# A float32 hybrid decoder trunk: state-space gates and products put in another order, attention in time halves, and the last projection in token layout

## The chip, the core and the metric

The kernel runs on one core of a Trainium2 chip. The metric is device time in microseconds, the median of several executions. Five engines work beside each other and each takes its instructions in order: TensorE (PE, matrix products into PSUM banks; PEld is its weight load), VectorE (DVE), ScalarE (ACT), GpSimd (POOL) and SyncE (SP), which here mostly issues DMA transfers.

## The reference, cut to what matters

256 tokens, width 1024, two layers, all float32:

```python
x = x + mamba2_mixer(rms_norm(x))          # state-space mixer, 8 groups of 4 heads
x = x + conv_ffn(rms_norm(x))              # 1024 -> 2 x 2816 -> 1024
k, v = shared_kv(rms_norm(x))              # 3 dilation groups (1, 4, 16), 2 KV heads each
x = x + dilated_attention(rms_norm(x), k, v)   # 8 heads a group, merged by softmax denominators
x = x + conv_ffn(rms_norm(x))
return rms_norm(x)

# mixer: z, xBC, dt = split(h @ w_in); xBC = silu(causal_conv4(xBC))
#   y = ssd(xs, dt, a, B, C) + d_skip * xs; y = group_norm(y * silu(z)); return y @ w_out
# ffn: u = causal_conv3(h @ w_up); return (silu(gate) * val) @ w_down
```

Three groups of keys with one softmax over them all is what the merge by denominators amounts to, and the kernel computes it so: a query has 256 columns for dilation 1 and 64 of its own residue class modulo 4 for each of the dilations 4 and 16, with a mask over all 384.

## The kernel before, in words

Activations stand as `[feature, token]`. Every large product is made of three one-pass products of rounded halves: weights `w = wh + wl` (`split`, L91 to L98: ScalarE rounds, L95, VectorE takes the difference, L97) and activations `x = xh + xl` (`hi_lo`, L168 and L169). `mm3` and `tile_a` (L242 to L244) have the weights stationary and 256 tokens moving; `tile_b` (L262 to L264) has 128 tokens stationary and 256 weight columns moving. Small products (state space, scores, values) are plain float32: each shows as two instructions in the trace.

`Weights` loads 1 MB pieces in the order of `seq` through three `raw` buffers and six pairs of `wh`/`wl`, one piece ahead. TensorE's order is the program's order (`manual_schedule`). The other engines' queues are put in order by a scheduler at build time, by readiness and program order; `seq(...)` chains some ScalarE passes.

Mixer: gates `z` (8 tiles of 256 columns, `z_mm`; three ahead of the groups and the rest as `ZAT` says), then for each of 8 groups two tiles each of `xs` and of B and C (`conv_mm`, 24 products a tile), their convolution (`conv_post`, VectorE taps L286) and Silu. A group's state-space work: `ssd_b` transposes `xs` (`px`) and makes `xdt`; `ssd_a` makes B x C (`pg`); `ssd_m` multiplies it into the decay `dec` (GpSimd); `ssd_c` makes `yo` and `py` and, over VectorE, GpSimd and ScalarE, the gated and normalised `y2` (`rs` is its scale); `ssd_d` transposes `y2` (`pt`) into the halves `yy`. `operands` makes the normalised halves `xnh`, `xnl`; `chunk_sums` the running sums (`pac`). `res_proj` multiplies by `w_out`, `w_down` or `w_o`, adds into `X` and feeds the next norm's operands (`Stream`); `hooks` runs leftover work between its steps; a step of `w_o`, or of the first four tiles of `w_out`, is three products of 256 columns. `late` are the operands that it takes last.

Attention: queries of the dilated groups stand by class `t % 4`. A head is three q tiles (`q_tile`, 24 products each), `scores` (two halves of 128 queries, 384 keys), softmax on VectorE and ScalarE, `p_transpose` (six 128-wide transposes) and `values`; in the loop over heads `p_transpose` and `values` run two heads behind, `scores` one:

```python
q_tile(h, hs[h], 0);  p_transpose(h - 2, hs[h - 2])
q_tile(h, hs[h], 1);  scores(h - 1, hs[h - 1])
q_tile(h, hs[h], 2);  values(h - 2, hs[h - 2])
```

The end: the last `w_down` leaves `[feature, token]`, its squares are summed over partitions by TensorE (`fss`, L934), 16 transposes turn it (`fin`, L927), four passes scale it and four DMAs write it.

Of the kernel before, what the change touches and what calls it, by code (L numbers as in the profile page):

```python
# [12 lines left out]
T = 256  # L13
D = 1024
# [17 lines left out]
_PRM = [("a_norm", 8), ("kv_norm", 8), ("b_norm", 8), ("ffn_norm0", 8), ("ffn_norm1", 8),  # L32
        ("final_norm", 8), ("ssm_norm", 16), ("dt_bias", 32), ("a_log", 32), ("dskip", 32),
# [3 lines left out]
_ATT = [("mask", 768), ("cos", 256), ("sin", 256), ("cosp", 256), ("sinp", 256)]  # L37
# [15 lines left out]
def trunk(ctx, tc, a, out):  # L53
# [46 lines left out]
    class Weights:  # L100


        def __init__(self):
# [5 lines left out]
            self.seq += [(("w_v", p), a["w_v"][p], 1024) for p in (1, 2, 0)]  # L109
# [27 lines left out]
        def begin(self, load, operand):  # L137

            _, src, m = self.seq[0]
            raw = wp.tile([128, 2048], F32, tag="raw", bufs=RB, name="raw")  # L140
            whl = [[wp.tile([128, 1024], F32R, tag=t, bufs=WB, name=t) for t in ("wh", "wl")]
                   for _ in range(2)]
            for i in range(4):
                c = slice(512 * i, 512 * i + 512)
                load(i)
                SP.dma_start(out=raw[:, c], in_=src[:, c])
            SP.dma_start(out=wdt.rearrange("p k h -> p (k h)"), in_=a["w_dt"])
            for i in range(4):
# [26 lines left out]

    class Stream:


        def __init__(self, ws):
            self.ws = ws  # L180
            self.h = []
            self.l = []
            for i in range(len(ws)):
# [20 lines left out]
    class Norm:  # L204


        def __init__(self, acc):
            self.acc = acc

        def stats(self):  # L210
            acc = self.acc
            ss = ps.tile([128, 512], F32, tag="t3", name="ss")
# [41 lines left out]
    def tile_b(po, units, xh, xl, n, c, ks=range(KT), clear=True, **kw):  # L254

        t = slice(c * 128, c * 128 + 128)
        kper = KT // len(units)
# [48 lines left out]
    def operands():  # L306
# [3 lines left out]
        for i in range(2):  # L310
            t = act.tile([128, 4, T], F32, tag=f"dec{2 + i}", name="xnt")
            for k in range(4):
                ACT.activation(out=t[:, k, :], in_=X[:, 4 * i + k, :], func=AF.Copy,
                               scale=P("a_norm")[:, 4 * i + k:4 * i + k + 1])
            for k in range(0, 4, 2):
                d, o = t[:, k:k + 2, :], slice(4 * i + k, 4 * i + k + 2)
                POOL.tensor_tensor(out=d, in0=d, in1=nm.row2, op=ALU.mult)
# [5 lines left out]
    W.fetch(2)  # L323
# [7 lines left out]
    sq += [wk.tile([128, 2 * T], F32, tag="zs", bufs=4, name="sq2") for _ in range(3)]  # L331
# [18 lines left out]
    def z_mm(g, c, **kw):  # L350
        st = sts[g]
        if "poz" not in st:
            st["poz"] = ps.tile([128, 2, T], F32, tag="t4", name="poz") if g == 2 else acc_bank()
            st["uz"] = W.get("w_z", g)
        tile_b(st["poz"][:, c, :], st["uz"], *xn[g > 2], 256, c, **kw)

    for k in range(0, KT, 2):
        for c in range(2):
            z_mm(0, c, ks=range(k, k + 2), clear=c == 0, skip_group_check=True)
# [5 lines left out]
    nm.stats()  # L365
    z_mm(1, 0)
    pdq = ps.tile([128, 512], F32, tag="t2", name="pdq")
    for c in range(2):
        PE.transpose(pdq[:, 32 * c:32 * c + 32], dtT[:, 128 * c:128 * c + 128], ident[0:32, 0:32])
    nm.bcast()  # L370
    z_mm(1, 1)
    col = nm.col
    W.fetch(4)
# [87 lines left out]

    def z_post(g):
        st, po = sts[g], sts[g]["poz"]
        zs = wk.tile([128, 2, T], F32, tag="zs", bufs=4, name="zs")
        if g < 3:
            for c in range(2):
                seq(out=zs[:, c, :], in_=po[:, c, :], func=AF.Silu, scale=col[:, c:c + 1])
        else:
            seq(out=zs, in_=po, func=AF.Silu)
        st["z"] = zs  # L470

    def ssd_a(g):
# [11 lines left out]

        if g == NG - 1:
            ssd_m(g)
# [28 lines left out]
    def ssd_c(g):  # L515
# [9 lines left out]
        y2 = wk.tile([128, 2, T], F32, tag="B", bufs=3, name="y2")  # L525
# [5 lines left out]
        POOL.tensor_tensor(out=y2, in0=xd, in1=st["z"], op=ALU.mult)  # L531
# [21 lines left out]
    for g in range(2):  # L553
        z_post(g)
    for c in range(2):
        z_mm(2, c)
    z_post(2)

    for g in range(NG):
        late = g > 1 and g - 1 not in ZAT  # L560
        conv_mm(g, "xs", 0)
        if late:
            ssd_c(g - 2)
        conv_mm(g, "xs", 1)
# [4 lines left out]
        conv_post(g, "xs")  # L569
        conv_silu(g, "xs")  # L570
        if g > 1 and not late:
            ssd_d(g - 2)
        conv_mm(g, "bc", 0)
# [3 lines left out]
        conv_mm(g, "bc", 1)  # L577
        conv_post(g, "bc")
        if g == 0:
            decay(0, sts[g]["end"])  # L580
# [486 lines left out]
```

## Time and profile before

| | |
|---|---|
| median of three runs | 794.57 us (794.43 to 795.48) |
| profiled execution | 796.08 us, span 794.3 us |
| mean granted TensorE clock | 0.993 |
| instructions | 14954 |

The span runs from the first to the last instruction of the profiled execution; its time has some 1.8 us beside the span. Busy time of TensorE runs from a product's start to its modelled end, so products that follow each other overlap; their cost is read from start to start. The granted clock is a share of 2.4 GHz.

### The profile page before, as it was taken

What the parts mean: (1) busy time and instruction counts of PE and PEld (TensorE: products, weight loads), DVE (VectorE), ACT (ScalarE), POOL (GpSimd) and SP (SyncE); (2) the same over time, 40 slices, a digit from 0 to 9 for tenths busy, and PEclk for the clock granted to TensorE, in tenths of its full rate; (3) what the DMA queues carried; (4) which work ended last, traced back from release to release, by engine and by line L of the source; (5) the groups of instructions that cost most, each with busy time, mean ns of one, the idle gap of its engine ahead of it and who ended that gap; (6) DMA issues with size and microseconds to landing.
All of it is one profiled execution on the core that took longest, in us unless ns stands there. A gap on an engine that the chain in (4) does not pass through costs nothing.

```text
span 794.3 us, 14954 instructions
## 1 busy us (share of the span) xinstructions
PE 774.3 (97%) x5992; PEld 742.7 (94%) x5992; DVE 619.5 (78%) x1004; ACT 478.6 (60%) x806; POOL 160.6 (20%) x141
## 2 busy tenths in 40 slices
PE   8999799999999999999999999999999999999997
PEld 7898799999989999999889999999999999999886
DVE  5888979788496999887677598878668999887551
ACT  7846568777375776655555446555466766565441
POOL 0323436543324400000011032211124300000010
PEclk9999989999999999999999999999999999999999
DMA  8484543363454366554556644334325465545521
GB/s 296 169 321 165 203 153 106 109 212 113 154 201 171 106 238 213 186 183 163 196 179 225 222 160 156 115 129 159 108 61 205 149 226 209 199 160 177 177 85 53
DMA packets 22886, 135.31 MB, mean 170 GB/s; under 512 B 2529, under 2 KB 4097, under 8 KB 8865
## 3 DMA queue, kind: packets, MB, share of 16 engines
q1 hardware_dynamic: 21616, 130.14, 47.0%
q10 hardware_dynamic: 1200, 4.23, 1.5%
q8 instruction: 47, 0.77, 0.4%
q14 instruction: 23, 0.18, 0.1%
HBM read 132.75 MB, written 1.61 MB: 169 GB/s over the span
## 4 chain that ended last, share of the span: by engine, by line
PE 75%; DVE 11%; POOL 4%; ACT 4%; issue 3%; DMA 2%; SPq 0%; DVEq 0%; ACTq 0%; POOLq 0%
PE po L242 15%; PE po L243 15%; PE po L244 15%; PE po L625 12%; PE po L627 6%; DVE wl L97 6%; PE po L633 4%; DVE cv L286 2%; PE s L854 1%; DVE xl L169 1%; POOL rs L537 1%; PE py L524 1%; PE op L888 1%; ACT wh L95 1%; PE op L892 1%
## 5 line engine op out<-in xcount | busy, mean ns | idle before, releaser
L97 DVE TENSOR_TENSOR wl<-raw,wh 128x1024 fp32r<-128x1024 f32 (+1 forms) x242 | 307.8, 1278 | 64.0 <-ACT wh L95 63.1
L95 ACT CAST wh<-raw 128x1024 fp32r<-128x1024 f32 (+1 forms) x242 | 247.7, 1034 | 170.5 <-PE po L243 87.0
L243 PE MATMUL po<-xnl,wh 128*128 128x256 f32 x800 | 227.0, 284 | 1.1 <-DVE xnl L319 1.1
L242 PE MATMUL po<-xnh,wh 128*128 128x256 f32 x800 | 227.0, 284 | 0.0
L244 PE MATMUL po<-xnh,wl 128*128 128x256 f32 x800 | 227.0, 284 | 0.0
L242 PEld LDWEIGHTS po<-xnh,wh 128*128 128x128 f32 x800 | 152.8, 191 | 0.3 <-issue 0.2
L243 PEld LDWEIGHTS po<-xnl,wh 128*128 128x128 f32 x800 | 151.2, 189 | 1.3 <-DVE xnl L319 1.3
L244 PEld LDWEIGHTS po<-xnh,wl 128*128 128x128 f32 x800 | 151.2, 189 | 0.1
L625 PE MATMUL po<-gp,wh 128*128 128x512 f32 x352 | 123.3, 393 | 0.0
L286 DVE SCALAR_TENSOR_TENSOR cv<-po,prm,cv 128x255 f32<-128x255 f32 (+2 forms) x232 | 105.8, 476 | 14.1 <-ACT cv L282 12.6
L242 PE MATMUL po<-xh,wh 128*128 128x256 f32 x400 | 115.0, 288 | 0.0
L243 PE MATMUL po<-xl,wh 128*128 128x256 f32 x400 | 113.2, 283 | 0.5 <-DVE xl L169 0.5
L244 PE MATMUL po<-xh,wl 128*128 128x256 f32 x400 | 113.0, 283 | 0.0
L627 PE MATMUL po<-gp,wl 128*128 128x256 f32 x352 | 98.5, 280 | 0.0
L625 PEld LDWEIGHTS po<-gp,wh 128*128 128x128 f32 x352 | 66.0, 187 | 15.4
L242 PEld LDWEIGHTS po<-xh,wh 128*128 128x128 f32 x400 | 76.3, 191 | 0.6
L243 PEld LDWEIGHTS po<-xl,wh 128*128 128x128 f32 x400 | 76.0, 190 | 0.7 <-DVE xl L169 0.7
L244 PEld LDWEIGHTS po<-xh,wl 128*128 128x128 f32 x400 | 75.9, 190 | 0.0
L627 PEld LDWEIGHTS po<-gp,wl 128*128 128x128 f32 x352 | 66.2, 188 | 0.0
L202 POOL TENSOR_TENSOR sqacc<-sqacc,sq 128x256 f32<-128x256 f32 x21 | 19.9, 946 | 217.0 <-ACT sq L201 216.7
L647 DVE TENSOR_TENSOR X<-po,X 128x256 f32<-128x256 f32 x52 | 20.9, 420 | 24.4 <-PE po L627 17.4
L202 POOL TENSOR_TENSOR facc<-facc,sq 128x256 f32<-128x256 f32 x6 | 4.5, 752 | 157.6 <-ACT sq L201 157.6
(207 smaller groups left out, 1270.4 us busy)
## 6 DMA issues: line engine op xcount, KB each, us to landing
raw<-w_up SPq DMA_DIRECT2D x44, 1024.0 KB, 4.8
raw<-w_down SPq DMA_DIRECT2D x16, 1024.0 KB, 4.8
raw<-w_xs SPq DMA_DIRECT2D x8, 1024.0 KB, 4.8
raw<-w_bc SPq DMA_DIRECT2D x8, 1024.0 KB, 4.8
raw<-w_out SPq DMA_DIRECT2D x8, 1024.0 KB, 4.8
raw<-w_q SPq DMA_DIRECT2D x8, 1024.0 KB, 5.1
raw<-w_z SPq DMA_DIRECT2D x7, 1024.0 KB, 6.2
raw<-w_down SPq DMA_DIRECT2D x8, 768.0 KB, 4.2
```

Source lines behind the costliest of these rows:

```text
L95: ACT.copy(out=wh[:, :n], in_=raw)
L97: DVE.tensor_tensor(out=wl[:, :n], in0=raw, in1=wh[:, :n].bitcast(F32), op=ALU.subtract)
L169: DVE.scalar_tensor_tensor(out=xl, in0=x, scalar=w, in1=xh.bitcast(F32), op0=ALU.mult, op1=ALU.subtract)
L202: POOL.tensor_tensor(out=acc, in0=acc, in1=sq, op=ALU.add)
L242: PE.matmul(po, lhsT=wh, rhs=xh, start=start, stop=False, **kw)
L243: PE.matmul(po, lhsT=wh, rhs=xl, start=False, stop=False, **kw)
L244: PE.matmul(po, lhsT=wl, rhs=xh, start=False, stop=stop, **kw)
L286: r = DVE.scalar_tensor_tensor(out=dst[:, i, s:], in0=u[:, i, :T - s], scalar=w[i][:, taps - 1 - s:taps - s], in1=dst[:, i, s:], op0=ALU.m ...
L625: PE.matmul(p.rearrange("p c t -> p (c t)"), lhsT=wh[:, c], rhs=y.rearrange("p c t -> p (c t)"), start=st, stop=False, skip_group_check=True)
L627: PE.matmul(p[:, 1, :], lhsT=wl[:, c], rhs=y[:, 0, :], start=False, stop=sp, skip_group_check=True)
L633: PE.matmul(p[:, o, :], lhsT=l[:, c], rhs=y[:, x, :], start=st and q == 0 and not o, stop=sp and q == 2, skip_group_check=True)
L647: DVE.tensor_tensor(out=x, in0=by_class(y) if perm else y, in1=x, op=ALU.add)
```

## The change

- Gates: 0 to 3 are made first, as two pairs of 512 columns from the unnormalised halves; 4 to 7 follow groups 1, 3, 5 and 7. VectorE makes the normalised operand in one pass a tile (ScalarE and GpSimd did in two).
- Mixer: `ssd_a` and `ssd_b` of group g-1 stand behind both B/C tiles of group g; `ssd_c(g-2)` and `ssd_d(g-3)` between them. `chunk_sums` stands behind the B/C tiles of group 0. Decays are loaded and exponentiated in pairs. `y2` lives in its group's `dec` buffer.
- V of the two dilated groups is one product 512 wide. Queries stand by class within each half of 128 tokens, keys in natural order (read with a stride of four columns); the first half's scores have 192 columns instead of 384 and two transposes instead of three; `values` handles two heads at once and writes its bank with a stride of four columns.
- `w_o`: hooks at 4, 7, 17 and 21 steps.
- The last projection has tokens stationary and 512 columns moving, so that its result stands as `[token, feature]`. `X` is transposed during the second up-projection (`turn`), the squares are summed by ScalarE's accumulator, and the outputs go out by two queues.

```diff
-ZAT = {0: 3, 2: 4, 5: 5, 6: 6, 7: 7}
-SSM = [("z", 0), ("z", 1), ("z", 2)]
+ZAT = {1: 4, 3: 5, 5: 6, 7: 7}
+SSM = [("z2", i) for i in range(4)]
 for _g in range(NG):
-    SSM += [("xs", _g), ("bc", _g)] + ([("z", ZAT[_g])] if _g in ZAT else [])
+    SSM += [("xs", _g), ("bc", _g)] + ([("z", ZAT[_g] - 4)] if _g in ZAT else [])
...
+    def z_pair(i, ks, po):
+        us = sum((W.get("w_z2", 2 * i + j) for j in sorted({k // 4 for k in ks})), [])
+        for k in ks:
+            for c in range(2):
+                tile_b(po[c], {k // 2: us[k // 2 - ks[0] // 2]}, *xn[0], 512, c, ks=[k])
...
+        tile_b(st["poz"][:, c, :], st["uz"], *xn[1], 256, c)
+    poz = [[ps.tile([128, 512], F32, tag=f"t{4 + c}", name="poz") for c in range(2)],
...
+        y2 = act.tile([128, 2, T], F32, tag=f"dec{g}", name="y2")
...
     for g in range(NG):
-        late = g > 1 and g - 1 not in ZAT
...
+        for i in range(2):
+            conv_mm(g, "xs", i)
+        conv_post(g, "xs")
+        conv_silu(g, "xs")
+        conv_mm(g, "bc", 0)
+        if g > 2:
+            ssd_d(g - 3)
+        if g > 1:
             ssd_c(g - 2)
-        conv_mm(g, "xs", 1)
+        conv_mm(g, "bc", 1)
...
+        if g and g % 2 == 0:
+            decay_load(g)
+            decay_load(g + 1)
+        if g % 2 == 0:
+            decay(g, sts[g]["end"])
+            decay(g + 1, sts[g]["end"])
         if g:
             ssd_b(g - 1)
             ssd_a(g - 1)
...
             z_mm(ZAT[g], 0)
-        if late:
-            ssd_d(g - 2)
-        if g in ZAT:
-            if g:
+            if g == NG - 1:
+                ssd_d(g - 2)
                 ssd_c(g - 1)
-            if g == NG - 1:
-                ssd_b(g)
             z_mm(ZAT[g], 1)
             z_post(ZAT[g])
...
-    def res_proj(w, nk, operand, late, S, facc=None, perm=False, first=2, hooks={}):
+    ssd_b(NG - 1)
+    ssd_a(NG - 1)
+    ssd_m(NG - 1)
...
+             first=4, hooks={20: lambda: ssd_d(NG - 2), 24: lambda: ssd_c(NG - 1), 52: lambda: ssd_d(NG - 1)})
...
+    def v_mm():
+        po = [acc_bank("vo").rearrange("p c f -> p (c f)") for _ in range(2)]
+        us = []
+        for ks in (range(4), range(4, 6), range(6, 8)):
+            if ks.start < 6:
+                us += W.get("w_v", ks.start // 4)
+            for c in range(2):
+                tile_b(po[c], us, xh, xl, 512, c, ks=ks)
+        return po
...
-                    PE.matmul(s[64 * r:64 * r + 64, 192 + 64 * g:256 + 64 * g], lhsT=q[:, g, t],
-                              rhs=KTt[g][:, kv, t], start=True, stop=True)
-            pm = wk.tile([128, 384], F32, tag="gs", name="pm")
+                o = s[:, n0:n].rearrange("p (c g i) -> p c g i", c=1 + c, g=2)[:, :, g - 1, :]
+                k = KTt[g][:, kv, :].rearrange("p (c i r) -> p c i r", c=2, r=4)
+                for r in range(4):
+                    PE.matmul(o[32 * r:32 * r + 32], lhsT=q[:, g, 128 * c + 32 * r:128 * c + 32 * r + 32], rhs=k[:, 0:1 + c, :, r],
+                              start=True, stop=True)
+            pm = wk.tile([128, 384], F32, tag="gs", name="pm") if c else P0[h % 2]
+            pv = pm[:, :n]
             mx = wk.tile([128, 1], F32, tag="mx", name="mx")
-            DVE.tensor_tensor_reduce(out=pm, in0=s[:, :384], in1=mask[:, c, :], scale=1.0, scalar=-3.0e38,
...
+    def values(h):
...
+        ov = op.rearrange("p h (c i r) -> p h c r i", c=2, r=4)
+        pv = pts.rearrange("p h (x r i) -> p h x r i", x=5, r=4)
+        for e in range(2):
+            PE.matmul(ov[:, e], lhsT=V0[:, 0, vc], rhs=pv[:, e, 0:3:2], start=e == 0, stop=False,
                       skip_group_check=True)
+        PE.matmul(ov[:, :, 1], lhsT=V0[:, 1, vc], rhs=pv[:, :, 3], start=False, stop=False,
+                  skip_group_check=True)
         for r in range(4):
-            t = slice(64 * r, 64 * r + 64)
-            PE.matmul(op[:, t], lhsT=Vs[:, r, vc], rhs=pts[:, 2, t], start=False, stop=r == 3,
-                      skip_group_check=True)
-        oh, ol = (OT[h // 2][:, h % 2, i, :] for i in range(2))
-        ACT.copy(out=oh, in_=op[:, :T])
-        DVE.tensor_tensor(out=ol, in0=op[:, :T], in1=oh.bitcast(F32), op=ALU.subtract)
...
         if h:
+            if h > 2 and h % 2:
+                values(h - 3)
             scores(h - 1, hs[h - 1])
...
+    res_proj("w_o", AH, lambda k: OT[k // 2][:, k % 2], [6, 7], S,
+             first=4, hooks={7: lambda: scores(AH - 1, hs[AH - 1]), 4: lambda: p_transpose(AH - 2, hs[AH - 2]),
                              17: lambda: p_transpose(AH - 1, hs[AH - 1]),
...
+                             21: lambda: values(AH - 2)})
...
+        for n in range(4):
+            PE.transpose(pt[:, n * 128:n * 128 + 128], X[:, 4 * f + n, c * 128:c * 128 + 128], ident)
+        ACT.copy(out=tok["x"][:, c, 512 * f:512 * f + 512], in_=pt)
...
+            def step(k, c):
+                wh, wl = us[k // 2]
+                o, t = slice(k % 2 * 512, k % 2 * 512 + 512), slice(128 * c, 128 * c + 128)
+                x = operand(k)
+                PE.matmul(po[c], lhsT=x[:, 0, t], rhs=wh[:, o], start=k == 0, stop=False)
+                PE.matmul(po[c], lhsT=x[:, 1, t], rhs=wh[:, o], start=False, stop=False)
+                PE.matmul(po[c], lhsT=x[:, 0, t], rhs=wl[:, o], start=False, stop=k == FT - 1)
```

## Rows read from the trace of the kernel before


**Rows 1.** The page, part 1: busy us, share of the span, instructions of each engine.
```profile
PE 774.3 (97%) x5992; PEld 742.7 (94%) x5992; DVE 619.5 (78%) x1004; ACT 478.6 (60%) x806; POOL 160.6 (20%) x141
```

**Rows 2.** Windows: busy us and instruction count of each engine, granted clock, DMA.
```profile
20.00:195.60 175.60, 165.40 (x1335) 162.26 (x1334) 150.82 (x229) 121.47 (x201) 72.07 (x49) 0.98 0.49 174
40.00:195.60 155.60, 147.25 (x1193) 144.98 (x1192) 133.09 (x197) 105.16 (x176) 65.24 (x44) 0.98 0.49 175
80.00:100.00 20.00, 15.66 (x126) 15.18 (x125) 18.49 (x25) 11.14 (x21) 9.60 (x6) 0.94 0.55 199
100.00:120.00 20.00, 20.00 (x150) 19.74 (x149) 16.07 (x25) 13.48 (x24) 6.67 (x5) 0.89 0.41 142
480.00:560.00 80.00, 80.00 (x678) 74.04 (x676) 63.58 (x144) 46.25 (x81) 12.77 (x13) 1.00 0.42 137
```

**Rows 3.** Waits of TensorE over the whole span: us in total, times, longest us.
```profile
PE pt L547 <- ACT y L539: 4.3, 1, 4.3
PE pg L476 <- ACT cv L381: 2.7, 2, 1.7
...
PE yo L519 <- POOL xdt L510: 1.2, 1, 1.2
PE po L243 <- DVE xnl L319: 1.1, 1, 1.1
...
PE pac L416 <- DVE smalls L406: 0.7, 1, 0.7
```

**Rows 4.** The chain of work that ended last, 20 to 45 us: start us, us, what.
```profile
22.16 6.67 POOL xnt L317 x4
```

**Rows 5.** Timeline of TensorE, second `w_down`: start us, us, operation.
```profile
776.18 0.39 PE L625 MATMUL po<-gp,wh 128*128 128x512 f32 x1
776.41 0.28 PE L627 MATMUL po<-gp,wl 128*128 128x256 f32 x1
776.53 0.39 PE L625 MATMUL po<-gp,wh 128*128 128x512 f32 x1
```

**Rows 6.** Timeline of TensorE, one attention head: scores, values, transposes, what follows.
```profile
519.38 0.59 PE L854 MATMUL s<-KTt,q 128*128 128x256 f32 x2
519.90 0.45 PE L859 MATMUL s<-KTt,q 128*64 128x64 f32 x8
520.28 0.70 PE L854 MATMUL s<-KTt,q 128*128 128x256 f32 x2
...
521.29 0.39 PE L242 MATMUL po<-xh,wh 128*128 128x256 f32 x1
...
524.27 1.03 PE L888 MATMUL op<-pts,V 128*128 128x256 f32 x4
525.13 1.00 PE L892 MATMUL op<-pts,Vs 128*128 128x64 f32 x8
525.94 0.37 PE L242 MATMUL po<-xh,wh 128*128 128x256 f32 x1
...
528.90 0.81 PE L878 MATMUL ptr<-cst,pm 128*128 128x128 f32 x6
```

**Rows 7.** Timeline of VectorE and ScalarE, the same head's softmax.
```profile
524.11 0.54 DVE L863 CUSTOM_DVE_ANT_0 pm<-s,mask 128x384 f32<-128x384 f32 x1
...
526.77 0.70 ACT L868 ACTIVATE pm<-pm,nb,sc 128x384 f32<-128x384 f32 x1
...
528.49 0.40 DVE L870 TENSOR_SCALAR pm<-pm,dn 128x384 f32<-128x384 f32 x1
```

**Rows 8.** Timeline of the end, behind the last product.
```profile
785.48 0.88 DVE L647 TENSOR_TENSOR X<-po,X 128x256 f32<-128x256 f32 x2 [1.22 <-PE po L627]
...
786.93 0.61 PE L934 MATMUL fss<-ones,sq 128*128 128x1 f32 x4 [0.27 <-ACT sq L656]
...
789.26 1.92 SPq L951 DMA_DIRECT2D out<-O  x4
```

**Rows 9.** DMA issues: operation, count, KB each, median us from issue to landing.
```profile
out<-O SPq DMA_DIRECT2D x4, 256.0 KB, 2.3
```

More of the change, by code (lines that the diff above doesn't have):

```diff
@@ L330, in trunk @@
     sq = [act.tile([128, 2 * T], F32, tag="dec5", name="sqa")]
-    sq += [wk.tile([128, 2 * T], F32, tag="zs", bufs=4, name="sq2") for _ in range(3)]
+    sq += [act.tile([128, 2 * T], F32, tag=f"dec{8 + i}", name="sq2") for i in range(3)]
     for i in range(4):
@@ L460, in conv_silu, with gate, z_pair_post @@
         seq(out=sts[g][n], in_=sts[g][n], func=AF.Silu)
-    def z_post(g):
[L463 to L470, printed above, removed]
+    def gate(g):
+        if g in (4, 5):
+            if g not in zp:
+                zp[g] = wk.tile([128, 2, T], F32, tag="C", name="zs")
+            return zp[g]
+        if g // 2 not in zp:
+            zp[g // 2] = wk.tile([128, 2, 512], F32, tag="zp", name="zp")
+        return zp[g // 2][:, :, g % 2 * 256:g % 2 * 256 + 256]
+    def z_pair_post(i):
+        gate(2 * i)
+        for c in range(2):
+            seq(out=zp[i][:, c, :], in_=poz[i][c], func=AF.Silu, scale=col[:, c:c + 1])
+    def z_post(g):
+        seq(out=gate(g), in_=sts[g]["poz"], func=AF.Silu)
     def ssd_a(g):
@@ L576, in trunk @@
             ssd_a(g - 1)
[L577 to L580, printed above, removed]
-            decay(1, sts[g]["end"])
-        if g:
             ssd_m(g - 1)
@@ L847, in q_tile @@
             q_rope(st["q"], st["sh"], po[:, :gs.stop - gs.start, :], gs)
+    P0 = [wk.tile([128, 1024], F32, tag="zp", name="p0") for _ in range(2)]
+    for p in P0:
+        POOL.memset(p[:, 192:256], 0.0)
     def scores(h, st):
@@ L881, in p_transpose @@
[L881 to L888 removed]
+            n = 256 + 128 * c
+            (DVE.tensor_copy if c else ACT.copy)(out=pts[:, h % 2, 256 * c:256 * c + n], in_=pt[:, :n])
+    def values(h):
+        kv, pts = h // 4, pair[h // 2]
+        vc = slice(kv * 128, kv * 128 + 128)
+        op = ps.tile([128, 2, T], F32, tag="t5", name="op")
+        ov = op.rearrange("p h (c i r) -> p h c r i", c=2, r=4)
+        pv = pts.rearrange("p h (x r i) -> p h x r i", x=5, r=4)
+        for e in range(2):
+            PE.matmul(ov[:, e], lhsT=V0[:, 0, vc], rhs=pv[:, e, 0:3:2], start=e == 0, stop=False,
@@ L896, in values @@
-        DVE.tensor_tensor(out=ol, in0=op[:, :T], in1=oh.bitcast(F32), op=ALU.subtract)
+            PE.matmul(ov[:, :, :, r], lhsT=Vs[:, r, vc], rhs=pv[:, :, 1::3, r], start=False,
+                      stop=r == 3, skip_group_check=True)
+        oh, ol = (OT[h // 2][:, :, i, :] for i in range(2))
+        ACT.copy(out=oh, in_=op)
+        DVE.tensor_tensor(out=ol, in0=op, in1=oh.bitcast(F32), op=ALU.subtract)
     hs = [{} for _ in range(AH)]
@@ L930, in trunk @@
-    turn(range(3))
-    ss = [acc_bank("fss") for _ in range(2)]
-    for i, q in enumerate((facc, lastsq[0])):
-        for c in range(2):
-            PE.matmul(ss[c][:, 0, 0:1], lhsT=q[:, c * 128:c * 128 + 128], rhs=ones[:, 0:1],
-                      start=i == 0, stop=i == 1)
-    turn(range(3, KT))
-    ms = wk.tile([128, 2], F32, tag="ms", name="ms")
-    for c in range(2):
-        DVE.tensor_scalar(out=ms[:, c:c + 1], in0=ss[c][:, 0, 0:1], scalar1=1.0 / D, scalar2=EPS,
-                          op0=ALU.mult, op1=ALU.add)
```

375 lines of the change are left out of this document (196 added, 179 removed).

## The prediction

> **What bounds the kernel now.** I read the share of busy time first: TensorE is busy 774 of 794.3 us and no other engine reaches 80% [rows 1]. So a change pays in three ways: fewer or cheaper TensorE instructions where TensorE never stops, fewer stops, a shorter end. The stretches show where it stops [rows 2]. Between 20 and 195.6 us, the state-space mixer, it is busy 165.40 of 175.60 us: 10.2 us idle. In 80 to 100 us it idles 4.34 us, and the granted clock, 1.00 (2.4 GHz) until then, averages 0.94 there and 0.89 in the next 20 us, with stretches at the lower level; 0.06 x 20 + 0.11 x 20 = 3.4 us more. The waits name the idle time [rows 3]: `pt` on the scaled `y` 4.3, `pg` on the convolved B/C 2.7, `yo` on `xdt` 1.2, the first normalised operand `xnl` 1.1, `pac` 0.7; together 10.0 of the 10.2. In 480 to 560 us, attention, TensorE is busy 80.00 of 80: there only its instruction count matters, as long as nothing new is late.
>
> **Mixer: the order of the products.** Before, `ssd_c(g-2)`/`ssd_c(g-1)`, `ssd_d` one group or one tile later, and `ssd_a`/`ssd_b` after half a B/C product. The work from `py` to `pt` is a relay of short passes on VectorE, GpSimd and ScalarE, each behind other work of its queue, and the products in hand ran out 4.3 us before it was through [rows 3]. The change puts `ssd_c(g-2)` into group g and its `ssd_d` one whole group later: four projection tiles of 24 products at 0.12 us [rows 5], 11.5 us, plus a gate tile pair (5.8 us) in every odd group lie between. `ssd_a(g-1)` moves behind both B/C products and is thereby 2.9 us and more later; `yo` (in `ssd_c`) gets 8.6 us behind `xdt`. `pac` moves from after 5.8 us of products to after 11.5 us. All five waits lose their place, and with the 4.3 us one the clock drop: at most 10.0 + 3.4 = 13.4 us.
>
> What is late next is VectorE. From 40 to 195.6 us it is busy 133.09 us [rows 2]; the change takes almost none of that away. Squeezed into 155.6 - 11 = 144.6 us VectorE would be at 92%, against 86% now and 18.49 of 20 in the stretch with the longest stall. Ahead of the first group it also gets eight products more: the chain shows four GpSimd multiplications in 6.67 us [rows 4], now eight VectorE ones at about 0.46 us (half of the 0.88 us that two 256-wide VectorE passes take [rows 8]), 3.7 us, queued among weight differences. Their cover grows: two pairs of gate tiles (96 products at 0.23) run ahead instead of three tiles (144 at 0.12), 22.1 against 17.3 us. I therefore keep 9.4 us of the 13.4 and give 4.0 back; the bounds are 13.4, and 2 if VectorE dictates the order. `ssd_d(7)` comes four steps before the late products instead of twelve: four steps are 4 x 3 x 0.12 = 1.4 us for a conversion chain of some 2 us: +0.5.
>
> **Wider products.** A 512-wide product takes 0.23 us from start to start, a 256-wide one 0.12 [rows 5]. Gates 0 to 3: 192 x 0.12 = 23.0 becomes 96 x 0.23 = 22.1. V for two dilated groups: 96 x 0.12 = 11.5 becomes 48 x 0.23 = 11.0. Last projection: 176 x (0.23 + 0.12) = 61.6 becomes 264 x 0.23 = 60.7. Together -2.3. The start needs 3 MB instead of 2 MB before pair 0 is through, but the products that wait for it take 11 us instead of 5.8: nothing for it either way. Wait positions of V move behind 8 us of products: nothing counted.
>
> **Attention, TensorE's side.** Values: now 4 instructions of 256 in 525.13 - 524.27 = 0.86 and 8 of 64 in 525.94 - 525.13 = 0.81 [rows 6], 1.67 us a head. Afterwards for two heads 6 instructions of 256 at 0.215 and 8 of 128 at 0.108 (half of 0.215, and not under the 0.101 of the 64-wide): 2.15 instead of 3.34, -1.2 for each of 4 pairs, -4.8. Transposes: 0.81 us for six with one latency is about 0.11 each; one fewer a head, -0.9. Scores: now 1.91 us from 519.38 to 521.29, in it 8 small instructions in 0.38 (519.90 to 520.28). Afterwards 16 small ones for each half, and the first half's wide product is half as wide (-0.2). If a small one costs what it does now, 16 x 0.0475 = 0.76, a head gains +0.5 us; if its cost halves with its columns and rows, it loses 0.25. Bounds +4.2 and -1.9; I take 0. Sum -5.7.
>
> All value products now write every fourth column of their bank and the small scores read every fourth column of K; no row shows a strided matmul, so the cost lies between nothing and a multiple f. I take f = 1: these are two-pass products that stream a column in 0.215/256 = 0.84 ns, twice the time of the 512-wide ones (0.23/512 = 0.45 ns), so the write side has slack. The Trainium skill speaks against it: "PSUM — Partial Sum Buffer", Specifications, says that a non-contiguous access pattern slows matmuls significantly. No row here shows that; by it the sum would go by rival C.
>
> **Attention, what is late.** From the end of a head's scores (521.29) to its last scaled probabilities (528.49 + 0.40) pass 7.6 us [rows 6, 7], although the work in it is short: the second half's maximum waits until 524.11, its exponential until 526.77. The cover is now two q tiles and a value block, and the second half's transposes start at 529.23: 0.3 us to spare. The change takes the value block out of this interval: 48 x 0.12 + 0.22 = 6.0 us. The first half's passes shrink from 384 to 192 columns, worth, by their columns, about 0.6 us of 0.54 + 0.70 + 0.40 [rows 7]. Deficit up to 7.0 - 6.0 = 1.0 us for each of six heads; head 6 is transposed at step 4 of w_o, 24 x 0.12 + 12 x 0.12 + 0.22 = 4.5 us behind its scores, deficit up to 2.5; head 7 up to 1; and the last pair's values stand 9 products (1.1 us) before the products that need them, up to 0.5. Together up to 10 us; the queue order of VectorE and ScalarE is new, and much of the 7.6 us is queue: half, +5.0. Attention nets -0.7.
>
> **End.** 16 transposes of X move into the up-projection, where TensorE never stops: 16 x 0.11 = +1.8. Behind the last product two adds take 0.88 us from 785.48 on, the first output is issued at 789.26, 3.8 us later, the four issues take 1.92 us, and the end is at 794.3, 8.8 us behind 785.48 [rows 8]; an output lands 2.3 us after its issue [rows 9]. Afterwards the square, its running sum, the power and the scaling stay in the chain, but the sum over partitions (TensorE, 0.61) goes, the first token half's output has been sent four microseconds earlier (18 products at 0.23), and the other half's two outputs are issued on two queues: 3.8 - 0.6 + 1.92/4 + 2.3 = 6.0, and 0.1 for a wait more. So -2.7, net -0.9.
>
> **Sum.** -9.4 + 0.5 - 2.3 - 0.7 - 0.9 = -12.8. The profiled execution took 796.08 (span 794.3 and 1.8 around it), 1.5 above the median of 794.57; the differences apply to either, so 794.6 - 12.8 = 781.8.
>
> **Rivals.**
> A. The softmax stalls come in full: the waits of 10 us eat the attention's gain. For it: 0.3 us of slack today. Against: the queue order is free. 781.8 + 5 = 786.8.
> B. VectorE becomes the bound of the mixer, only 2 of 13.4 us come back: 781.8 + 7.4 = 789.2. For it: 92%. Against: it reached 92% in 80 to 100 us even with the waits of the old order.
> C. Slower: strided products. Value pairs (4 x 2.15 = 8.6) and small scores (1.91 less two wide products of 0.3 and 0.6 and the gaps between them, 0.9 x 8 heads = 7.2) make 15.8 us; at f = 2 the time is 797.6, and from f = 1 + 12.8/15.8 = 1.8 it is no gain. This is what the page named above would do here; the rows bear it out nowhere.
> D. Everything hides, no stall in attention and all 13.4 in the mixer: 781.8 - 5 - 4 = 772.8.
>
> **Chances.** Forecast (776 to 787 by its own bounds) 46%, A 18, B 14, C 10, D 12. The range takes D, A and B in and leaves C out: 772 to 794, A and B together ending at its top. Under 0.2% (1.6 us) this kernel can't be told from unchanged: faster 84%, same 4% (A with B), slower 12% (C and the worst of A with B).
>
> **What would show it.** Mixer: no `pt` wait over 1 us, clock 1.00 between 80 and 120, w_out's first product 10 us earlier; if not, VectorE at 95% with TensorE waiting for convolved tiles (B). Attention: the value block of a pair 2.2 us, scores 1.9 us a head; waits of `ptr` on the scaled probabilities are A, a value block of 4 us is C. End: 6 us behind the last product. The prediction fails if stalls move to a place that I count as covered, the operands ahead of group 0 or the late products of w_o above all.

## The result, and the profile after

The changed kernel takes 784.38 us (median of four runs, 783.55 to 784.8) against 794.85 for the kernel before on the same chip: ratio 0.9866, 95% interval 0.9849 to 0.9883, so 10.5 us less. The forecast was 781.8 (772 to 794). Its profiled execution has a span of 783.0 us, 11.3 less than that of before (whose profiled execution, 796.08 us, lies 1.2 above its median), and a mean granted clock of 0.992 (0.993 before). The page, part 1 (busy us, share, instructions), to be read beside [rows 1]:

```profile
PE 765.2 (98%) x5832; PEld 725.0 (93%) x5832; DVE 604.9 (77%) x1008; ACT 469.4 (60%) x793; POOL 140.5 (18%) x134
```

TensorE is still the engine to watch. Its waits over the whole span (us in total, times, longest us) answer to [rows 3]:

```profile
PE po L270 <- DVE cv L314: 2.5, 2, 2.0
PE pt L587 <- ACT y L579: 2.1, 1, 2.1
PE poz L290 <- ACT wh L167: 1.5, 2, 0.9
PE ptr L923 <- DVE pm L909: 1.4, 4, 0.4
...
PE py L564 <- POOL dec L530: 0.4, 1, 0.4
```

The `pt` wait of 4.3 us, `pg`, `yo`, `xnl` and `pac` are gone. In their place stand a wait for a convolved tile, which is not among the waits of the kernel before, and another wait of `pt`, in another group. What each stage took is read from the first product of the next one in the two traces:

| stretch (by first products; `w_o` and the last projection end with their last) | before | after | change | forecast |
|---|---|---|---|---|
| start to first up-projection (mixer, gates, `w_out`) | 241.80 | 237.08 | -4.7 | -9.8 |
| first feed-forward block | 189.34 | 189.15 | -0.2 | 0 |
| V, K and the first four query tiles (to the first scores) | 50.81 | 49.67 | -1.1 | -0.5 |
| attention from the first scores on, and `w_o` | 113.19 | 109.14 | -4.0 | -0.7 |
| second up-projection (holds the turn of X) | 128.55 | 130.28 | +1.7 | +1.8 |
| last projection, to its last product | 61.47 | 60.37 | -1.1 | -0.9 |
| last product to end | 9.14 | 7.32 | -1.8 | -2.7 |

The change was 10.5 us where 12.8 were forecast, but two of the terms were off by more than that difference, in opposite directions. The mixer gave half of what was forecast, the attention over five times as much.

**Where the mixer stops.** The windows (busy us and instructions of PE, PEld, DVE, ACT and POOL, granted clock, DMA share, GB/s), beside [rows 2]:

```profile
100.00:120.00 20.00, 17.96 (x137) 17.73 (x137) 18.41 (x27) 13.93 (x24) 4.74 (x6) 0.91 0.57 211
...
160.00:180.00 20.00, 17.41 (x140) 16.52 (x139) 18.62 (x31) 15.58 (x28) 12.35 (x9) 1.00 0.44 149
180.00:200.00 20.00, 20.00 (x143) 19.89 (x143) 11.18 (x14) 9.80 (x18) 5.74 (x5) 0.83 0.30 98
```

Two stops of some 2 us, each followed by a stretch at the lower clock: 0.09 x 20 + 0.17 x 20 = 5.2 us more. The first one on TensorE's timeline (start us, us, operation):

```profile
107.93 0.27 PE L272 MATMUL po<-xnh,wl 128*128 128x256 f32 x1
110.24 0.36 PE L270 MATMUL po<-xnh,wh 128*128 128x256 f32 x1 [2.04 <-DVE cv L314]
...
111.82 0.42 PE L270 MATMUL po<-xnh,wh 128*128 128x256 f32 x1
112.04 0.42 PE L271 MATMUL po<-xnl,wh 128*128 128x256 f32 x1
```

From 111.82 on products start 0.21 us apart instead of 0.12: the clock is at its lower level (1.2 GHz; the granted clock is 0.50 from 111.8 to 114.4 us). VectorE's timeline ahead of the stop:

```profile
102.08 1.22 DVE L98 TENSOR_TENSOR wl<-raw,wh 128x1024 fp32r<-128x1024 f32 x1
103.21 0.48 DVE L314 SCALAR_TENSOR_TENSOR cv<-po,prm,cv 128x254 f32<-128x254 f32 x1
103.60 1.22 DVE L98 TENSOR_TENSOR wl<-raw,wh 128x1024 fp32r<-128x1024 f32 x1
104.73 0.87 DVE L314 SCALAR_TENSOR_TENSOR cv<-po,prm,cv 128x253 f32<-128x253 f32 x2
105.58 2.60 DVE L98 TENSOR_TENSOR wl<-raw,wh 128x1024 fp32r<-128x1024 f32 x1
108.10 0.47 DVE L314 SCALAR_TENSOR_TENSOR cv<-po,prm,cv 128x254 f32<-128x254 f32 x1
108.50 1.21 DVE L98 TENSOR_TENSOR wl<-raw,wh 128x1024 fp32r<-128x1024 f32 x1
109.63 0.47 DVE L314 SCALAR_TENSOR_TENSOR cv<-po,prm,cv 128x253 f32<-128x253 f32 x1
```

Four weight differences (L98) stand between the taps (L314) of the tile whose bank TensorE needs, and VectorE has no pause there. The third takes 2.60 us instead of 1.22. Beside it runs GpSimd's decay multiply, 2.59 us from 104.50 to 107.09, and the difference ends at 108.18, 1.1 us behind it:

```profile
104.50 2.59 POOL L530 TENSOR_TENSOR dec<-dec,gs 128x1024 f32<-128x1024 f32 x1 [2.54 <-ACT gs L524]
```

The Trainium skill, "SBUF — State Buffer", "SBUF: two separate sides", says that a VectorE pass with two SBUF inputs and a GpSimd operation lock each other out of a shared pair of ports for a whole instruction; the row agrees, since 107.09 and 1.22 us for the difference itself make 108.3.

VectorE was already late here: further ahead, the waits of VectorE and of ScalarE between 30 and 110 us show a transfer.

```profile
DVE dec L474 <- DMA dec<-rows: 4.4, 2, 4.2
```
```profile
ACT dec L416 <- POOL dec L477: 4.6, 2, 3.9
```

The running sums now stand behind both B/C products of group 0, so the decays' transfer starts later. VectorE waits for it at 54 to 58 us, GpSimd masks behind VectorE, and ScalarE waits for the mask with the next group's convolutions queued behind. In the kernel before VectorE did not wait for this transfer at all. The second stop, from TensorE, VectorE and GpSimd:

```profile
177.84 0.94 PE L587 MATMUL pt<-cst,y 128*128 128x128 f32 x4 [2.12 <-ACT y L579]
...
179.62 3.44 PE L564 MATMUL py<-xdt,dec 128*128 128x64 f32 x16 [0.40 <-POOL dec L530]
```
```profile
173.99 2.40 DVE L98 TENSOR_TENSOR wl<-raw,wh 128x1024 fp32r<-128x1024 f32 x2
176.31 0.16 DVE L575 TENSOR_SCALAR sm<-sm 128x2 f32<-128x2 f32 x1
```
```profile
176.54 0.70 POOL L577 TENSOR_TENSOR rs<-sm,nhalf 128x2 f32<-128x2 f32 x1 [2.38 <-DVE sm L575]
177.21 2.35 POOL L530 TENSOR_TENSOR dec<-dec,gs 128x1024 f32<-128x1024 f32 x1
```

In group 7 `ssd_d(5)` stands between the halves of the gate tile. The scale `rs` that it needs waited for a 0.16 us pass on VectorE that stood behind two weight differences; GpSimd had been idle 2.38 us, and its decay multiply for `py` is late for the same reason.

**Attention.** The timeline of a pair's values, and of one head's scores (answering to [rows 6]):

```profile
499.23 1.03 PE L935 MATMUL op<-pts,V 128*128 128x256 f32 x4
500.09 0.59 PE L937 MATMUL op<-pts,V 128*128 128x256 f32 x2
500.53 1.05 PE L940 MATMUL op<-pts,Vs 128*128 128x128 f32 x8
501.42 0.39 PE L890 MATMUL s<-KTt,q 128*128 128x128 f32 x2
...
512.58 0.39 PE L890 MATMUL s<-KTt,q 128*128 128x128 f32 x2
512.89 0.42 PE L897 MATMUL s<-KTt,q 128*32 128x32 f32 x16
513.25 0.70 PE L890 MATMUL s<-KTt,q 128*128 128x256 f32 x2
513.88 0.65 PE L897 MATMUL s<-KTt,q 128*32 128x64 f32 x16
514.46 0.39 PE L270 MATMUL po<-xh,wh 128*128 128x256 f32 x1
```

A pair's values take 501.42 - 499.23 = 2.19 us (2.15 forecast), although every product writes with a stride. A head's scores take 514.46 - 512.58 = 1.88 us.

**The end**, answering to [rows 8] and [rows 9]: TensorE's last product, then VectorE, ScalarE, GpSimd and the DMA.

```profile
775.69 0.39 PE L1029 MATMUL fo<-wl,gp 128*128 128x512 f32 x1
776.12 0.76 DVE L990 TENSOR_TENSOR xt<-fo,xt 128x256 f32<-128x256 f32 x2 [1.11 <-PE fo L1029]
...
778.01 0.55 POOL L1013 TENSOR_TENSOR fcol<-ms,nhalf 128x1 f32<-128x1 f32 x1 [3.53 <-DVE ms L994]
778.60 0.72 ACT L1014 ACTIVATE wf<-wf,fcol 128x512 f32<-128x512 f32 x1 [1.12 <-POOL fcol L1013]
...
779.35 0.34 ACTq L1017 DMA_DIRECT2D out<-wf  x1
```

From the adds (776.12) to the issue pass 3.2 us, as forecast (3.8 - 0.6); behind the issue 3.7 us to the span's end, where 2.8 were counted.

### The profile page after: what moved, and what is told of

Read it like the earlier page. It is cut to its first block, busy times and chain, and to the rows that moved or that the text cites. A ratio compares the mean times of both kernels' runs of the same rounds, so it can differ in the third digit from the quotient of the medians.

```text
span 783.0 us, 14619 instructions
## 1 busy us (share of the span) xinstructions
PE 765.2 (98%) x5832; PEld 725.0 (93%) x5832; DVE 604.9 (77%) x1008; ACT 469.4 (60%) x793; POOL 140.5 (18%) x134
## 4 chain that ended last, share of the span: by engine, by line
PE 88%; DVE 5%; ACT 2%; DMA 2%; issue 1%; POOL 1%; SPq 0%; POOLq 0%; DVEq 0%; ACTq 0%
PE po L270 17%; PE po L271 17%; PE po L272 17%; PE po L659 7%; PE po L667 4%; PE po L661 4%; PE fo L1029 2%; PE fo L1027 2%; PE fo L1028 2%; PE py L564 2%; DVE wl L98 2%; DMA raw<-w_z 1%; DMA dec<-rows 1%; PE s L897 1%; PE po L290 1%
## 5 line engine op out<-in xcount | busy, mean ns | idle before, releaser
L96 ACT CAST wh<-raw 128x1024 fp32r<-128x1024 f32 (+1 forms) x238 | 245.1, 1041 | 191.6 <-PE po L271 100.7
L98 DVE TENSOR_TENSOR wl<-raw,wh 128x1024 fp32r<-128x1024 f32 (+1 forms) x238 | 295.1, 1246 | 75.2 <-ACT wh L96 74.2
L314 DVE SCALAR_TENSOR_TENSOR cv<-po,prm,cv 128x255 f32<-128x255 f32 (+2 forms) x232 | 106.1, 477 | 6.2 <-ACT cv L310 3.5
L659 PE MATMUL po<-gp,wh 128*128 128x512 f32 x176 | 61.4, 392 | 0.0
L230 POOL TENSOR_TENSOR sqacc<-sqacc,sq 128x256 f32<-128x256 f32 x21 | 21.7, 1033 | 211.3 <-ACT sq L229 211.0
L661 PE MATMUL po<-gp,wl 128*128 128x256 f32 x176 | 49.3, 280 | 0.0
L659 PEld LDWEIGHTS po<-gp,wh 128*128 128x128 f32 x176 | 33.0, 187 | 7.5
L1027 PE MATMUL fo<-wh,gp 128*128 128x512 f32 x88 | 34.5, 392 | 0.0
L1029 PE MATMUL fo<-wl,gp 128*128 128x512 f32 x88 | 34.5, 392 | 0.0
L1028 PE MATMUL fo<-wh,gp 128*128 128x512 f32 x88 | 34.5, 392 | 0.0
```

Of the source, the lines that this page charges most:

```text
L96: ACT.copy(out=wh[:, :n], in_=raw)
L98: DVE.tensor_tensor(out=wl[:, :n], in0=raw, in1=wh[:, :n].bitcast(F32), op=ALU.subtract)
L314: r = DVE.scalar_tensor_tensor(out=dst[:, i, s:], in0=u[:, i, :T - s], scalar=w[i][:, taps - 1 - s:taps - s], in1=dst[:, i, s:], op0=ALU.m ...
L659: PE.matmul(p.rearrange("p c t -> p (c t)"), lhsT=wh[:, c], rhs=y.rearrange("p c t -> p (c t)"), start=st, stop=False, skip_group_check=True)
L661: PE.matmul(p[:, 1, :], lhsT=wl[:, c], rhs=y[:, 0, :], start=False, stop=sp, skip_group_check=True)
L1027: PE.matmul(po[c], lhsT=x[:, 0, t], rhs=wh[:, o], start=k == 0, stop=False)
```

## The experiments

All times are medians on a chip that also ran the kernel before in the same session (794.97, 795.20, 795.43 and 795.15 us in the four sessions).

**One part at a time.** Three kernels have one part of the change each, the rest as before.

> The kernel before with the mixer's part of the change alone (gates first in two 512-wide pairs, operands by VectorE, the new order of the groups, decays in pairs, y2 in its group's decay buffer); attention and the last projection as before. Theory 1 (the shares read from the two traces stage by stage): about -4.7 us against before, 790.1. Theory 2 (the prediction's own terms: -9.4 for the order, +0.5 for the last hook, -0.9 for the gates): -9.8, 785.0. Rival (the mixer's gain stands or falls with the other parts, which share its buffers): under 2 us either way from before.

> The kernel before with the attention's part alone (V 512 wide, queries by class within each half, 192 columns for the first half, values for two heads at once with strided reads and writes, hooks of w_o). Theory 1 (stages of the two traces: V -1.1, heads -2.6, w_o -1.4): about -5.1 us against before, 789.7. Theory 2 (the prediction: V -0.5, attention -0.7): -1.2, 793.6. Rival (the attention's gain in the changed kernel came from a later or earlier start of its transfers): between the two, with a head's values not at 2.2 us a pair.

> The kernel before with the last projection's part alone (X turned in the second up-projection, 512 weight columns moving, squares by ScalarE's accumulator, outputs by two queues). Theory 1 (stages of the two traces: turn +1.7, products -1.1, tail -1.8): about -1.2 us against before, 793.6. Theory 2 (the prediction: +1.8 -0.9 -2.7): -1.8, 793.0. Rival (the turn hides and the tail gives its 2.7): -3.6.

Measured: mixer 788.89 (ratio 0.9925, 0.991 to 0.994), -6.1; attention with V 790.11 (0.9938, 0.9921 to 0.9955), -4.9; last projection 794.69 (0.9995, 0.9986 to 1.0005), -0.3, not to be told from nothing. They sum to -11.2 against -10.5 together, so the parts hardly depend on each other, and the shares of the table (-4.7, -5.1, -1.2) hold within 1.4 us: the mixer was over-estimated, the attention under-estimated. The mixer alone has the same two waits (`po` on `cv` 2.2, `pt` on `y` 2.1); that it gave more than its share fits the clock, which in its profile stays at 1.00 from 100 to 120 us, where the changed kernel shows 0.91.

**The second stop: group 7.**

```diff
             z_mm(ZAT[g], 0)
-            if g == NG - 1:
-                ssd_d(g - 2)
-                ssd_c(g - 1)
             z_mm(ZAT[g], 1)
             z_post(ZAT[g])
+    ssd_d(NG - 3)
+    ssd_c(NG - 2)
```

> The changed kernel, but in the last group the transposes of y2 of group 5 and the state products of group 6 stand behind both halves of the gate tile instead of between them, 2.9 us later. Theory 1 (what costs the end of the mixer is too little cover in front of these two, 2.3 us of waiting for y, 1 us for the decay, and the lower clock after it, 0.17 x 20 = 3.4 us): no wait of pt or py over 0.5 us, clock 1.00 from 160 to 190 us, 4 to 6 us less than the changed kernel, 778.5 to 780.5. Rival (VectorE is late whatever the order): the wait goes on to the first steps of w_out or to the products behind ssd_c, less than 1.5 us gained.

Measured 779.74 (0.9802, 0.9787 to 0.9816), 4.6 us less than the changed kernel. The waits and windows of TensorE:

```profile
PE po L270 <- DVE cv L314: 2.9, 2, 2.3
...
PE pt L587 <- ACT y L579: 0.8, 1, 0.8
...
PE py L564 <- POOL dec L530: 0.2, 1, 0.2
```
```profile
180.00:200.00 20.00, 19.16 (x158) 18.67 (x158) 13.11 (x18) 9.30 (x21) 8.80 (x8) 1.00 0.35 118
```

The stop in group 7 and the lower clock behind it are gone; 2.9 us of products ahead of the two steps were enough. The 0.8 us left stand at the next `pt`, inside `w_out`. The first stop stays.

**The first stop: three ways at VectorE's queue, and one at K's layout.** All on e4.

```diff
# e5: the first two decays one tile later
+        if g == 1:                                # behind conv_silu(1, "xs")
+            for i in range(2):
+                decay(i, sts[g]["end"])
+            seq(out=ea, in_=acs[:, 32:96], func=AF.Exp)
+            for i in range(2):
+                decay_exp(i)
...
-        if g % 2 == 0:
+        if g and g % 2 == 0:                      # decay and decay_exp of the other pairs
# e6: in conv_post
+        with tc.high_priority():
             st["end"] = conv(cv, u, ..., 4)
# e7: in conv_post
-            st["end"] = conv(cv, u, ..., 4)
+            st["end"] = conv(cv, u, ..., 3)
# e8: in values and scores
-ov = op.rearrange("p h (c i r) -> p h c r i", c=2, r=4)
+ov = op.rearrange("p h (c r i) -> p h c r i", c=2, r=4)
-k = KTt[g][:, kv, :].rearrange("p (c i r) -> p c i r", c=2, r=4)
+k = KTt[g][:, kv, :].rearrange("p (c r i) -> p c i r", c=2, r=4)
```

> As e4_group7_order, and the first two decays (and the exponential of ea) are subtracted, masked and exponentiated behind the xs products of group 1 instead of behind the B/C products of group 0; their loads stay where they are. Theory 1 (the wait of 2.3 us for a convolved tile near 108 us has its cause at 52 to 62 us: VectorE waits 3.7 us for the decays' DMA and 2.5 us for ScalarE, which waits 4.5 us for the first masked decay with convolutions queued behind it, and the lag is carried until the three accumulator banks are used up): these waits, the wait of po near 108 and the lower clock behind it (0.09 x 20 us) go, 3.5 to 4.1 us less than e4, 775.6 to 776.2. Theory 2 (VectorE's load alone, 92% between 100 and 120 us): the wait of po stays over 1.5 us, under 1 us gained. Rival: the decay multiply of group 0 comes late and py waits for it in group 2, 1 to 3 us more than e4.

Measured 776.38 (0.9758, 0.9744 to 0.9773), 3.4 less than e4. Its waits of TensorE and its VectorE queue:

```profile
PE po L270 <- DVE cv L314: 0.5, 1, 0.5
```
```profile
103.08 2.60 DVE L98 TENSOR_TENSOR wl<-raw,wh 128x1024 fp32r<-128x1024 f32 x1
...
107.12 0.47 DVE L314 SCALAR_TENSOR_TENSOR cv<-po,prm,cv 128x253 f32<-128x253 f32 x1
```

VectorE no longer waits for the decays' transfer. The same passes stand in the same order as in the changed kernel, the 2.60 us one too, but everything is 2.5 us earlier (105.58 and 109.63 there). So the four weight differences alone make a stop of 0.5 us; the 2 us come from a lag of 2.5 us ahead of them, which came from waiting for a transfer 50 us earlier. The edit moved VectorE's, GpSimd's and ScalarE's share of these decays together, so which of their waits carried how much of the lag is not shown.

> As e4_group7_order, and the mixer's convolutions are given priority when the queues are built, so that fewer weight differences stand between the taps of a tile. Theory 1 (late decays): the convolutions of 52 to 62 us still stand behind the wait, under 1.5 us gained or lost. Theory 3 (the four weight differences of 1.2 to 2.6 us between the taps near 102 to 110 us cause the wait): the wait of po near 108 goes, 3 to 4 us less than e4. Rival: the weight differences come late instead and TensorE waits for wl, slower than e4 by 2 us or more.

Measured 789.21 (0.9914, 0.9898 to 0.9931), 9.5 more than e4. The wait for a convolved tile is gone, as theory 3 has it, and `pt` waits instead, which none of the expectations had; behind its two stops the clock falls too (0.83 in 120 to 140 us, 0.74 in 180 to 200):

```profile
PE pt L588 <- ACT y L580: 7.1, 2, 4.6
```

> As e4_group7_order, but the mixer's convolution leaves out its fourth tap (s = 3): two of six VectorE passes of each pair of tiles, 32 x 0.4 = 13 us of VectorE's 129 us between 35 and 188.5 us. Theory 2 (VectorE's load bounds what the order can give): every wait of the mixer for convolved tiles and for y goes, 4 to 6 us less than e4, and more than e5 gives. Theory 1 (late decays): the waits of VectorE and ScalarE at 52 to 62 us stay, the lag is made up sooner, and the gain is no more than that of e5, 3.5 to 4.1 us.

Measured 785.36 (0.9874, 0.9849 to 0.99), 5.6 more than e4 with less work. The queues were ordered anew when it was built, and the stops moved: `py` for the decay 2.4 us in three waits, `pt` 2.6 in two. As a test of VectorE's load it decides nothing, except that 13 us less work there did not make up for what the new order cost.

> As e4_group7_order, but the value products write their bank in contiguous runs of 32 columns and the small score products read K in contiguous runs of 32 instead of with a stride of four (this leaves out the permutation of tokens, the number of products and columns is the same). Theory 1 (a stride of four columns costs these two-pass products nothing, f = 1): within 0.3 us of e4, first value product to last of a pair 2.2 us in both. Rival (strided access slows them, f over 1.2): 15.8 x 0.2 = 3 us less than e4 or more.

Measured 776.50 (0.9759, 0.974 to 0.9778). Each expectation was right for one half of the edit. The value products take the same in both layouts: 379 ns an instruction of 256 columns, 275 of 128, and 2.2 us a pair. The small score products of one half, first e4, then e8:

```profile
472.41 0.65 PE L896 MATMUL s<-KTt,q 128*32 128x64 f32 x16
```
```profile
469.97 0.43 PE L896 MATMUL s<-KTt,q 128*32 128x64 f32 x16
```

From start to start all 256 small score products sum to 7.4 us in e4 and 5.0 in e8: 2.4 us come from reading K with a stride, none from writing the values with one. The other 0.8 us of the 3.2 gained fits the clock, which in e8's profile did not fall behind a stop of 2.1 us (1.00 in 100 to 120 us, 0.91 in e4); e8's four runs spread from 774.91 to 777.77 us, so this remainder is argued, not shown.

**Undoing the place of the sums.**

```diff
-        conv_mm(g, "bc", 1)
         if g == 0:
             chunk_sums()
             decay_load(0)
             decay_load(1)
+        conv_mm(g, "bc", 1)
```

> As e4_group7_order, but the running sums and the first two decay loads stand between the two B/C products of group 0, 2.9 us earlier, as this part of the change is undone; the decays keep their place. Theory 1 (the late start of the decays causes the wait near 108 us): VectorE's wait for the decays' DMA falls from 3.7 us to about 1, the wait of po near 108 from 2.3 us to under 1, TensorE waits up to 0.7 us for the time steps as in the kernel before; 1 to 3.5 us less than e4, 776.3 to 778.7. Rival (it is the place of the decays in the queues, not their loads): within 0.7 us of e4.

Measured 781.90 (0.9834, 0.9818 to 0.985), 2.2 more than e4: both expectations missed. The early waits went as theory 1 has it (VectorE waits for no decay transfer), but the wait near 108 us grew:

```profile
PE po L270 <- DVE cv L314: 4.1, 2, 3.9
```

The queues show a likely reason. GpSimd's timeline of e12 and then of e5, whose order here is also that of e4:

```profile
85.17 2.39 POOL L530 TENSOR_TENSOR dec<-dec,gs 128x1024 f32<-128x1024 f32 x1
87.52 1.70 POOL L577 TENSOR_TENSOR rs<-sm,nhalf 128x2 f32<-128x2 f32 x1
```
```profile
82.56 0.72 POOL L577 TENSOR_TENSOR rs<-sm,nhalf 128x2 f32<-128x2 f32 x1
...
85.00 2.40 POOL L530 TENSOR_TENSOR dec<-dec,gs 128x1024 f32<-128x1024 f32 x1 [1.73 <-ACT gs L524]
```

In e12 the decay multiply is queued ahead of the tiny `rs` in two groups in which e4 and e5 have `rs` first. ScalarE waits 3.65 us for `rs` at 89.25 and again here, with roundings of weights behind it:

```profile
108.82 0.91 ACT L579 ACTIVATE y<-y,rs 128x256 f32<-128x256 f32 x2 [3.03 <-POOL rs L577]
```

VectorE waits 2.07 us for these roundings, and the last tap comes at 111.83. The lag was taken out at one place and came back at another, by an order that no line of the edit names. That this order is the cause was not tested by itself: in later groups e4 has waits of 3.0 us for `rs` too (126.48 and 162.63), without a stop of TensorE.

**What can be added.** Keys written by class, the operands as they were, and the transposes of the probabilities later:

```diff
# e9, in k_post for the dilated groups (the rope tables by class, scores as in e8)
-        DVE.tensor_tensor(out=kt, in0=po, in1=nm.row2, op=ALU.mult)
+            for i in range(2):
+                DVE.tensor_tensor(out=kt[:, i, :].rearrange("p (c r i) -> p c i r", c=2, r=4),
+                                  in0=po[:, i, :].rearrange("p (c i r) -> p c i r", c=2, r=4),
+                                  in1=nm.row.rearrange("p (c i r) -> p c i r", c=2, r=4), op=ALU.mult)
# e10, in the loop over heads, for heads before the last
-        if h > 1:
-            p_transpose(h - 2, hs[h - 2])
         q_tile(h, hs[h], 1)
+        if 1 < h < AH - 1:
+            p_transpose(h - 2, hs[h - 2])
...
         q_tile(h, hs[h], 2)
+        if 2 < h < AH - 1 and h % 2:
+            values(h - 3)
# e11, in operands
-                for q in range(k, k + 2):
-                    DVE.scalar_tensor_tensor(out=t[:, q, :], in0=X[:, 4 * i + q, :], ...)
+            for k in range(4):
+                ACT.activation(out=t[:, k, :], in_=X[:, 4 * i + k, :], func=AF.Copy, ...)
...
+                POOL.tensor_tensor(out=d, in0=d, in1=nm.row2, op=ALU.mult)
```

> As e5_decays_one_tile_later, and the keys of the two dilated groups are written by class within each half (VectorE permutes them once, two passes a product), so that the small score products read them in contiguous runs of 32 columns. Theory 1 (in e8 the 256 small score products took 5.0 us from start to start, in e4 7.4, the value products the same in both: only the strided read costs): 2.4 us less than e5, 774.0. Rival (the small products' time is that of their weight loads and e8's other 0.8 us came from a clock that did not fall): under 1 us.

Measured 773.94 (0.9736, 0.9722 to 0.9751), 2.4 less than e5, as reckoned from e8.

> As e9_k_by_class, and the transposes of the probabilities of heads 0 to 4 stand one q tile later (2.9 us), with the pair's values behind the third q tile. Theory 1 (the waits of ptr for the scaled probabilities, four times 0.4 to 0.57 us, are all that is left of the softmax stalls): 1.5 to 2.1 us less than e9, no wait of ptr before the last two heads. Rival (the queues of VectorE and ScalarE shift with it and the values or the scores wait instead): no gain.

Measured 772.37 (0.9717, 0.9702 to 0.9731), 1.6 less than e9; of the four waits of `ptr` one of 0.5 us is left. This is the fastest version, 12.0 us below the changed kernel and 23.1 below the kernel before.

> As e5_decays_one_tile_later, but the normalised operands are made as in the kernel before: ScalarE scales, GpSimd multiplies by the row, two tiles at a time. Theory 1 (eight VectorE products, 3.7 us, cost nothing, and GpSimd's four of 1.7 us would end behind the gates): the first xs product waits for xnl, 0.5 to 3 us more than e5. Theory 2 (VectorE is at its limit, 19.5 of 20 us between 100 and 120): 3.7 us of VectorE come free, 0.5 to 1 us less than e5.

Measured 777.19 (0.9776, 0.9759 to 0.9792), 0.8 more than e5. The first `xs` product comes 0.6 us later (35.27 against 34.71), and the wait for a convolved tile is back at 1.6 us. Taking 3.7 us of work off VectorE did not make its queue earlier: the last tap ahead of that wait starts at 108.71 instead of 107.12. Why it is later by more than the 0.6 us is not shown.

## Why the prediction was right, and where it was not

The direction and the range held, and the terms of the end were right within 1 us; but that the total came within 2.6 us is luck, since two larger errors offset each other. The range helps little: it is 22 us wide and ends 0.6 us below the unchanged time.

**The mixer, the term that was mis-sized.** "All five waits lose their place" was right up to group 7, where `pt` waits 2.1 us, and 13.4 us was about the right size of what there was to gain. With both new stops taken out (e5) the first up-projection starts at 228.32 us instead of 241.80, 13.5 us earlier, for 13.4 and 0.9 of the wider gates. The step that failed is "I therefore keep 9.4 us of the 13.4 and give 4.0 back": the stage gave 4.7 us, so some 9 were given back, by two stops that cost 2.0 and 2.1 us by themselves and 5.2 through the clock behind them. e4 and e5 recovered 8.0 us. The prediction's own signs say the same: `pt` waits over 1 us, the clock is 0.91 between 100 and 120 us, and `w_out`'s first product comes 3.7 us earlier (188.50 against 192.22) instead of 10; in e5 it comes at 178.48. The 4.0 was reckoned from VectorE's mean share, and this was the wrong measure. Between 35 and 188.5 us VectorE is busy 129.43 of 153.50 us, 84%, under the 92% forecast; but it idled early, behind a transfer, and was at 92% and 93% in the two stretches that stop. "`pac` moves from after 5.8 us of products to after 11.5 us" was costed as a gain only; what its delay does to the decays' transfer, and who is queued behind that, was not followed. Of group 7's exception to the new order nothing was said.

**Rival B** was half right. Its sign appeared, TensorE waiting for convolved tiles, but VectorE's sum of work is not the bound: e11 took work off it and lost 0.8 us, e5 took none off and won 3.4. What the runs point to is the order in three queues; that VectorE's load would bind next is not excluded, since each test of it (e7, e11) changed an order too. That the decays' transfer is the origin of the lag is shown for this order of the queues by the shift of 2.5 us in e5; e12 shows that removing it is not enough when the order changes with it. Which orders arise from which edit is not settled, and neither is what the same work would take with the queues held fixed.

**The last hook of the mixer** (+0.5) cost nothing: no wait of `pt` stands there in any of these traces. **V** gave 1.1 instead of 0.5 us; its 512-wide products start 0.227 us apart, and 96 x 0.12 - 48 x 0.227 = 0.6 of it is that. The rest was not taken apart.

**Attention, TensorE's side.** Values: from start to start 13.4 us before, 8.7 after, -4.7 (-4.8 forecast). Transposes 4.6 to 3.8, without their waits (-0.9 forecast). Scores, forecast 0 within +4.2 and -1.9: 15.5 to 14.9. In this zero a cost of 2.4 us for the strided reads was hidden; without it they would have given 3.0.

**Attention, what is late**, forecast +5.0 of up to 10, was 2.1 us: four gaps of 0.4 to 0.57 at the second half's transposes, and 0.2 at the late products of `w_o`. This is the second term that was mis-sized: "half, +5.0" was a guess at how much of the softmax stays uncovered, and it makes 2.9 of the 3.3 us by which the attention was under-estimated. Rival A in full is refuted, and e10 shows that all but one of these gaps could be covered.

**Rival C**, strided access. f was to be 1.8 over 15.8 us of products to cost the gain. It is 1.0 for the writes and 7.4/5.0 = 1.5 for the small reads alone. The Trainium skill's rule that the prediction weighed ("PSUM — Partial Sum Buffer", Specifications) isn't borne out by these products: 379 and 275 ns in both layouts, and the measurement decides. For the reads the Trainium skill, "SBUF — State Buffer", "Door 1: The DMA port swizzle", says that each access to a new line of 16 bytes costs extra, and also that float32 can be strided by four for free. These rows fit the first and not the second: from start to start a small product takes 7.4/256 = 0.029 us with that stride and 5.0/256 = 0.020 without it.

**The end.** Turn +1.7 (+1.8). The products -1.1 (-0.9). The tail -1.8 (-2.7): the chain was right to 0.1 us, and the missing 0.9 lies from the last issue on, where 3.7 us pass and 2.3 with 0.5 for the issue were counted. The rows of before already had this: there the fourth issue ends at 789.26 + 1.92 = 791.18 and the span 3.1 us later [rows 8], here 3.3 us later; 2.3 us is only the way to landing. e3 by itself measures -0.3 with an interval of -1.1 to +0.4, so the whole part is worth little.

## What to carry to other kernels

A mean busy share tells whether an engine can be a bound, not where its queue will be late: follow one late transfer through the instructions queued behind it, up to the buffer that runs out. An edit that moves one step also moves every transfer that step issues, and where the queues are ordered at build time it may reorder others. When a total agrees, compare the stages before trusting the reasons.

## What was not expected of the hardware

- A stop of the same length does not always cost the clock: behind 2.0 us (the changed kernel) and 2.3 us (e4) the window of 100 to 120 us shows 0.91, behind 2.2 us (e1) and 2.1 us (e8) it shows 1.00. The runs of one kernel differ in this too: e8's two runs with a mean clock of 0.998 took 774.91 and 775.60 us, the two with 0.993 and 0.996 took 777.40 and 777.77.
- Reading the moving operand with a stride of four float32 columns costs 9 ns, from start to start, on an instruction of 32 or 64 columns (2.4 us over 256 of them), while writing PSUM with the same stride costs nothing on instructions of 128 and 256.
